# A two-layer encoder step: which engine begins the prompt attention's loads, and where one mixer keeps its cached values

## The chip, the core and the metric

The kernel runs on one core of a Trainium2 chip. The core has a matrix engine (PE), a vector engine (DVE), a scalar engine (ACT), a general engine (POOL) and a synchronising engine (SP) that here only begins transfers. Each works through its own list of instructions in order; a transfer between DRAM and on-chip memory (SBUF) is begun by an instruction in one of these lists and then carried out by the core's 16 DMA engines. The metric is the device time of one launch in microseconds, lower is better.

## The reference

Two request groups go through the same weights: one prompt of 512 frames and eight samples of 16 frames with 256 cached frames each. Layer 0 mixes by an RWKV recurrence beside forgetting attention (`fox`), layer 1 by chunk-band attention (`chunk`) beside an HGRN recurrence; a gated convolution network follows each. Cut to the attention:

```python
def fox_prompt(q, k, v, logf):                 # mixer 0, 8 heads of 64, 512 frames
    cum = jnp.cumsum(logf.astype(jnp.float32), axis=1)
    ...
        s = jnp.einsum('bqhd,bkhd->bhqk', qi, k) * ATTN_SCALE \
            + fi.transpose(0, 2, 1)[..., None] - f_keys      # f_keys: cum of the keys
        s = jnp.where(pi[:, None] >= pos[None, :], s, -jnp.inf)
        p = jax.nn.softmax(s, axis=-1)
        return jnp.einsum('bhqk,bkhd->bqhd', p, v)
def chunk_attn_prompt(q, k, v, rel_bias):      # mixer 1: the same with a bias by distance
    bias = rel_bias[:, jnp.clip(rel, -REL_CLIP, REL_CLIP) + REL_CLIP]
    s = jnp.einsum('bcqhd,bckhd->bchqk', qc, kb) * ATTN_SCALE + bias[None, None]
    ...
def chunk_attn_sample(q, k, v, ck, cv, rel_bias):   # 16 new frames over 256 cached ones
    keys = jnp.concatenate([ck, k], axis=1)
    vals = jnp.concatenate([cv, v], axis=1)
    ...
def trunk(x, c, P, cache):
    for layer in range(DEPTH):                 # DEPTH = 2
        h = rmsnorm(x) * (1.0 + scale) + shift
        y, st = ab_mixer(h, ...) if layer % 2 == 0 else cd_mixer(h, ...)
        x = x + gate * y
        h = rmsnorm(x) * (1.0 + scale) + shift
        y, buf_new = conv_ffn(h, ...)
        x = x + gate * y
```

All values are 32-bit floats.

## The kernel before

**Matrix products with weights.** `linear` (L334) takes the weights of a layer in steps of up to 512 KB. A step is loaded by SP into a ring of four tiles named `wraw` (L344, L345). ACT casts the tile to a rounded part `whi` (L348), DVE forms the remainder `wlo` (L349), and PE makes three products for each pair of weight block and half of the frames (L359, output `lin`). These are the bulk of the program.

**Prompt attention.** `attn_prompt` (L1027) goes through the eight heads in four pairs. Q, K and V of a mixer have been written to DRAM in parts. For each pair, twelve loads of 64 x 512 values (128 KB, L1072) bring Q and the two parts of K for both heads, one load (L1073) brings V, and `prep` brings one table per head: in mixer 0 the running sums of `logf`, spread over the partitions (L956, into `room`), in mixer 1 the distance bias `cbp` (L1406), which DVE then negates (L1407) and POOL masks in a corner (L1408). Before the change POOL begins the twelve and SP begins the V load and the tables. Every tile here exists once (`room`, L1012; the trace calls some of these tiles `ra`, the others `room`), so the next pair's loads wait until the last reader of the present pair is done. Within a pair, `front` makes the scores (PE, `qk`, L1044), adds the table and takes the extreme (DVE, L1045), the exponential (ACT, L1046) and the normalisation (DVE, L1047 and L1048); `turn` transposes the probabilities (PE, `ptr`, L1054) and copies them (ACT, L1055); `back` multiplies by V (PE, `av`, L1061), and DVE copies the result (L1063). The V of a pair is transposed once (PE, `vt`, L1084). `todo` lets `turn` and `back` run one block behind `front`, so that the last blocks of a pair are finished in the next pair.

**Sample attention.** `attn_sample` (L1093) takes the eight samples one after another. `front` loads a sample's cached keys `kc` and values `vc`, 512 KB each, from SP (L1121, L1122) into the same ring of four `wraw` tiles that the weights use, and makes the scores (`sqk`, L1129 and L1130). `back` runs one sample later and is the last to read `vc` (`sav`, L1152; its scaling on DVE is L1154, its transpose `syt` L1156).

**The recurrence of mixer 0.** For each stretch of frames it inverts a small triangular matrix by some 30 short POOL instructions that follow each other (L683 and L685, tiles `Tt` and `Ttmp`), with the operands going to DRAM and back before and after (tile `d`).

**What sets the order.** The program gives work in lanes with priorities, and a scheduler that simulates the engines' times sorts every engine's list (the class `Streams` holds the lanes). A change of who begins a transfer therefore moves other instructions too. In mixer 0 the prompt attention, the sample attention and the recurrence run beside the input product (`lin`), and beyond its end; in mixer 1 prompt attention, sample attention and HGRN run beside it.

**How a transfer is waited for.** Transfers begun by SP and ACT share a set of eight completion counters in this program (the ones begun by POOL have eight others); a transfer that reuses a counter is begun only when the one before it on that counter has landed. SP, ACT or POOL, whichever begins it, waits in its list, and what stands behind waits with it.

Of the kernel before, what the change touches and what calls it, by code (L numbers as in the profile page):

```python
# [9 lines left out]
F32 = mybir.dt.float32  # L10
# [9 lines left out]
NP = 512  # L20
# [119 lines left out]
H = (slice(0, 64), slice(64, 128))  # L140
# [374 lines left out]
def mixer0(tc, A, k):  # L515
    nc = tc.nc
    V, S, G, T, dma, mm, fm, P, C = k.V, k.S, k.G, k.T, k.dma, k.mm, k.fm, k.P, k.C
# [9 lines left out]
    with tc.tile_pool(name="mx", bufs=1) as mp:  # L527
# [419 lines left out]
        cumd = dr.tile([8, NP], F32, name="cumd")  # L947
# [5 lines left out]
        S.activation(ncq.rearrange("p a b -> p (a b)"), pst[:, 0:32], AF.Copy, scale=-1.0)  # L953

        def prep(head, t):
            dma(t, cumd[head].partition_broadcast(128))  # L956
            return t

        def addend(head, i, t, o):
# [67 lines left out]
def attn_prompt(A, k, mp, ydr, slot, dq, dk, dv, prep, addend, room):  # L1027
# [40 lines left out]
    for p in range(4):  # L1068
        for h in range(2):
            for (t, d) in ((qs[h], (dq[0], dq[1])), (kh[h], (dk[0], dk[0])), (kl[h], (dk[1], dk[1]))):  # L1070
                for g in range(2):
                    G.dma_start(t[H[g]], d[g][p][H[h], :NP])  # L1072
        dma(v, dv[p][:, :NP])  # L1073
        for h in range(2):
            prep(2 * p + h, cb[h])
        for i in range(4):
            front(p, i, 0)
            if todo is not None:
                turn(todo[1], 1)
                back(*todo)  # L1080
            if i == 0:
                ps = fm("vt", 1)
                for j in range(4):
                    T.transpose(ps[:, 128 * j:128 * j + 128], v[:, 128 * j:128 * j + 128], ident)  # L1084
                S.copy(vt.rearrange("p a b -> p (a b)"), ps)
            front(p, i, 1)
            turn(i, 0)
            todo = (p, i)
# [1 line left out]
    back(*todo)  # L1090


def attn_sample(A, k, mp, ydr, slot, dq, dk, dv, sprep, sbias, sadd, ck, cv, tags, bank):  # L1093

    V, S, G, T, dma, _, C, act = k.V, k.S, k.G, k.T, k.dma, k.lm, k.C, k.act
    ident = k.ident
# [19 lines left out]
    def front(b):  # L1116
        s_ = ss[b % 2]
        kc = k.wp.tile([128, 1024], F32, tag="wraw", name="kc", bufs=4)
        vc = k.wp.tile([128, 1024], F32, tag="wraw", name="vc", bufs=4)
        kc, vc = kc.rearrange("p (a t) -> p a t", a=4), vc.rearrange("p (a t) -> p a t", a=2)  # L1120
        dma(kc, A[ck][b])  # L1121
        dma(vc, A[cv][b])  # L1122
        ps = bank("sqk")
        if sbias is not None:
            sbias(b, ps)
        for p in range(4):
            lhs = qbd[:, p, b].rearrange("p h t -> p (h t)")
            o = ps[32 * p:32 * p + 32]
            T.matmul(o[:, 0:256], lhs, kc[:, p, :], start=sbias is None, stop=sbias is None, tile_position=(0, 32 * p))  # L1129
            T.matmul(o[:, 256:384], lhs, ks[:, p, :], start=sbias is None, stop=True, tile_position=(0, 32 * p))  # L1130
        st = mp.tile([128, 2], F32, tag="sst", name="sst", bufs=3)
        if sadd is not None:
            sadd(b, ps, s_, st)
            src = s_
        else:
            V.tensor_reduce(st[:, 0:1], ps[:, :384], axis=AX.X, op=ALU.min)
            src = ps[:, :384]
        S.activation(s_, src, AF.Exp, scale=-1.0, bias=st[:, 0:1], accum_out=st[:, 1:2])
        V.reciprocal(st[:, 1:2], st[:, 1:2])
        return b, s_, vc, st  # L1140
# [33 lines left out]
def mixer1(tc, A, k):  # L1174
# [13 lines left out]
    with tc.tile_pool(name="hx", bufs=1) as mp:  # L1188
# [214 lines left out]
        V.tensor_copy(C["win"][:, 112:128], sbt[:, 256:272])  # L1403

        def prep(head, t):
            dma(t, A["cbp"][head])  # L1406
            V.tensor_scalar(t, t, -1.0, None, op0=ALU.mult)  # L1407
            G.memset(t[0:64, 448:512], BIG)  # L1408
            return t
# [6 lines left out]
            V.tensor_tensor_reduce(s_[:, 256:384], ps[:, 256:384], C["win"][:, 112 - 16 * b:240 - 16 * b], 1.0, st[:, 1:2],  # L1416
                                   op0=ALU.add, op1=ALU.min, accum_out=st[:, 0:1])

        sample = k.stepper(1, attn_sample(A, k, mp, ydr, 0, cqs, cks, cv, lambda r: None, None, sadd, "c_ck", "c_cv", k.tags[0], mm), ln=1)
        lin([0, 1, 2, 3, 4, 5, 6, 7], (1,), sample)  # L1420
        sample.rest()
        with k.lane(1):
# [122 lines left out]
```

## Time and profile before

| | before |
|---|---|
| runs, us | 2049.37, 2043.58, 2048.91 (median 2048.91) |
| profiled execution, us | 2047.2 |
| its span, us | 2045.4 |
| granted TensorE clock, mean | 0.977 |
| PE / DVE / ACT / POOL busy | 94% / 59% / 46% / 26% |

The span runs from the first to the last record of the profiled execution; the other 1.8 us lie around it. The granted clock is a share of full speed (2.4 GHz); 0.977 is a mean over the span. A busy share is that of all instructions of an engine that have a duration; instructions that begin a transfer are not counted in it.

### The profile page before, as it was taken

The numbers are of one execution on the slowest core, as the hardware profiler recorded it, in microseconds if no ns is written. First come the engines' busy times: TensorE is split into PE (matmuls) and PEld (weight loads), VectorE is DVE, ScalarE is ACT, GpSimd is POOL, SyncE is SP. The second block draws the span as 40 slices with busy tenths as digits, with TensorE's granted clock in tenths as the row PEclk, the third lists the DMA queues.
The fourth block names the chain that finished last, engine by engine and source line by source line (L and its number), as shares of the span: only waits on it lengthen the run. The fifth ranks groups of instructions, "written<-read, shape, count | busy, mean of one in ns | idle before, by whom it ended". The sixth has DMA issues, their size and how long they took to land. (4 is left out here: it accounts for less than half of the span.)

```text
span 2045.4 us, 42529 instructions
## 1 busy us (share of the span) xinstructions
PE 1932.5 (94%) x16860; PEld 1746.0 (85%) x16860; DVE 1216.1 (59%) x2485; ACT 943.9 (46%) x1877; POOL 524.6 (26%) x1090
## 2 busy tenths in 40 slices
PE   5999998998999999999999999988999999999997
PEld 2877787765797899999999888877889999999997
DVE  3755665786686454454558515776678653454455
ACT  4634433454456451451446425565637642452454
POOL 1425453535021120121112201443222321121112
PEclk7999999998999999999999999999999999999998
DMA  8464436376535532222236775456634322222223
GB/s 314 146 224 122 158 116 188 92 180 167 160 121 184 198 112 78 78 66 79 79 102 214 242 247 175 124 141 185 218 95 152 108 75 81 73 67 78 83 80 124
DMA packets 144663, 282.52 MB, mean 138 GB/s; under 512 B 39769, under 2 KB 80065, under 8 KB 144465
## 3 DMA queue, kind: packets, MB, share of 16 engines
q1 hardware_dynamic: 136784, 267.22, 41.3%
q0 software_dynamic: 7680, 12.59, 2.9%
q8 instruction: 133, 2.18, 0.4%
q14 instruction: 66, 0.53, 0.1%
HBM read 247.69 MB, written 32.07 MB: 137 GB/s over the span
## 5 line engine op out<-in xcount | busy, mean ns | idle before, releaser
L359 PE MATMUL lin<-hi,whi 128*128 128x320 f32 x2272 | 716.1, 315 | 16.8 <-ACT whi L348 8.9
L359 PE MATMUL lin<-hi,wlo 128*128 128x320 f32 x2272 | 713.2, 314 | 5.8 <-DVE wlo L349 5.7
L359 PE MATMUL lin<-lo,whi 128*128 128x320 f32 x2272 | 711.7, 313 | 0.0
L349 DVE TENSOR_TENSOR wlo<-wraw,whi 128x1024 fp32r<-128x1024 f32 (+1 forms) x272 | 334.3, 1230 | 349.5 <-ACT whi L348 348.6
L348 ACT CAST whi<-wraw 128x1024 fp32r<-128x1024 f32 (+1 forms) x272 | 279.6, 1028 | 505.0 <-PE lin L359 373.4
L359 PEld LDWEIGHTS lin<-hi,whi 128*128 128x128 f32 x2272 | 431.0, 190 | 40.2 <-ACT whi L348 12.3
L359 PEld LDWEIGHTS lin<-hi,wlo 128*128 128x128 f32 x2272 | 430.8, 190 | 21.1 <-DVE wlo L349 9.0
L359 PEld LDWEIGHTS lin<-lo,whi 128*128 128x128 f32 x2272 | 430.9, 190 | 6.2 <-issue 2.7
L359 PE MATMUL lin<-gh,whi 128*128 128x320 f32 x704 | 218.1, 310 | 2.9 <-ACT whi L348 1.8
L359 PE MATMUL lin<-gl,whi 128*128 128x320 f32 x704 | 217.5, 309 | 0.6 <-DVE gl L451 0.6
L359 PE MATMUL lin<-gh,wlo 128*128 128x320 f32 x704 | 217.4, 309 | 0.6 <-DVE wlo L349 0.5
L433 POOL COPY cvo<-u 128x2 f32<-128x2 f32 x88 | 82.8, 941 | 383.4 <-ACT u L431 383.4
L394 DVE SCALAR_TENSOR_TENSOR x<-lin,ada_cm,x 128x192 f32<-128x192 f32 (+1 forms) x160 | 76.8, 482 | 143.5 <-PE lin L359 142.7
L359 PEld LDWEIGHTS lin<-gh,whi 128*128 128x128 f32 x704 | 132.0, 188 | 4.6 <-ACT whi L348 2.8
L359 PEld LDWEIGHTS lin<-gl,whi 128*128 128x128 f32 x704 | 132.1, 188 | 1.3 <-DVE gl L451 1.1
L359 PEld LDWEIGHTS lin<-gh,wlo 128*128 128x128 f32 x704 | 132.0, 188 | 1.4 <-DVE wlo L349 1.1
L399 POOL TENSOR_TENSOR x<-x,rs 128x128 f32<-128x128 f32 x80 | 49.7, 622 | 304.6 <-DVE rs L397 290.9
L437 DVE SCALAR_TENSOR_TENSOR t<-u,pp,t 128x656 f32<-128x656 f32 x88 | 79.3, 901 | 27.2 <-ACT t L436 26.6
L251 PE MATMUL ada<-wada,csT 128*32 128x256 f32 x768 | 70.2, 416 | 19.6 <-DMA wada<-in_ada_w_dram 19.3
L1294 POOL TENSOR_TENSOR d<-d,q 128x160 f32<-128x160 f32 (+1 forms) x48 | 41.7, 869 | 182.0 <-ACT d L1293 182.0
L359 PE MATMUL lin<-yh,whi 128*128 128x320 f32 x256 | 81.4, 321 | 5.5 <-DVE eL L1258 2.3
L436 ACT ACTIVATE t<-u,pp 128x656 f32<-128x656 f32 x88 | 82.6, 939 | 7.2 <-ACT u L432 0.4
(389 smaller groups left out, 3091.3 us busy)
## 6 DMA issues: line engine op xcount, KB each, us to landing
wraw<-in_w_up_dram SPq DMA_DIRECT2D x100, 512.0 KB
wada<-in_ada_w_dram SPq DMA_DIRECT2D x96, 512.0 KB
wraw<-in_w_cd_dram SPq DMA_DIRECT2D x44, 512.0 KB
wraw<-in_w_dn_dram SPq DMA_DIRECT2D x48, 448.0 KB
wraw<-in_w_ab_dram SPq DMA_DIRECT2D x40, 512.0 KB
wraw<-in_w_dn_dram SPq DMA_DIRECT2D x16, 512.0 KB
wraw<-in_w_abo_dram SPq DMA_DIRECT2D x12, 512.0 KB
wraw<-in_w_cdo_dram SPq DMA_DIRECT2D x12, 512.0 KB
```

What stands on the lines that cost most here:

```text
L251: T.matmul(ps[32 * j:32 * j + 32, 0:256], csT[:, kk, :], w[:, j * 256:(j + 1) * 256], start=kk == 0, stop=kk == KD - 1, tile_position=(0, ...
L348: S.copy(wh[:, :w], r[:, :w])
L349: V.tensor_tensor(wl[:, :w], r[:, :w], wh[:, :w].bitcast(F32), op=ALU.subtract)
L359: T.matmul(ps[:, 0:HF], w[:, (j * nk + kk) * 128:(j * nk + kk + 1) * 128], a(h, kk), start=c == 0, stop=c == 3 * nk - 1)
L394: V.scalar_tensor_tensor(xx[:, :npr], ps[:, :npr], m[:, 16 + o, 0:1], xx[:, :npr], op0=ALU.mult, op1=ALU.add)
L399: G.tensor_tensor(xx[:, npr:], xx[:, npr:], t.rearrange("p b t -> p (b t)"), op=ALU.add)
L433: G.tensor_copy(cvo[:, o, 0, :], u[:, NP:NP + 2])
L436: S.activation(t, u[:, 2:], AF.Identity, scale=pp[:, ow + 88 + o:ow + 89 + o], bias=pp[:, ob + o:ob + o + 1])
L437: V.scalar_tensor_tensor(t, u[:, 1:UW - 1], pp[:, ow + 44 + o:ow + 45 + o], t, op0=ALU.mult, op1=ALU.add)
L1294: G.tensor_tensor(dv[:, :, h2:], dv[:, :, h2:], xq[:, :, h2:], op=ALU.mult)
```

## The change

The twelve L1072 loads of each pair, its V load and its two tables are begun by ACT instead of POOL and SP, in both mixers: 96 loads leave POOL, 8 V loads and 16 tables leave SP, and ACT's list gets 120 instructions. The `bitcast` only matches the type of the destination. In mixer 1 the cached values `vc` of the samples get two tiles of their own (8 KB in each partition) and no longer pass through the `wraw` ring; the keys `kc` stay there. The amount of data is the same. From L1094 on the line numbers of the changed program are one higher.

```diff
--- before.py
+++ after.py
@@ -953,7 +953,7 @@
         S.activation(ncq.rearrange("p a b -> p (a b)"), pst[:, 0:32], AF.Copy, scale=-1.0)
 
         def prep(head, t):
-            dma(t, cumd[head].partition_broadcast(128))
+            S.dma_start(t, cumd[head].partition_broadcast(128))
             return t
 
         def addend(head, i, t, o):
@@ -1069,8 +1069,8 @@
         for h in range(2):
             for (t, d) in ((qs[h], (dq[0], dq[1])), (kh[h], (dk[0], dk[0])), (kl[h], (dk[1], dk[1]))):
                 for g in range(2):
-                    G.dma_start(t[H[g]], d[g][p][H[h], :NP])
-        dma(v, dv[p][:, :NP])
+                    S.dma_start(t[H[g]].bitcast(F32), d[g][p][H[h], :NP])
+        S.dma_start(v, dv[p][:, :NP])
         for h in range(2):
             prep(2 * p + h, cb[h])
         for i in range(4):
@@ -1090,7 +1090,7 @@
     back(*todo)
 
 
-def attn_sample(A, k, mp, ydr, slot, dq, dk, dv, sprep, sbias, sadd, ck, cv, tags, bank):
+def attn_sample(A, k, mp, ydr, slot, dq, dk, dv, sprep, sbias, sadd, ck, cv, tags, bank, own=False):
 
     V, S, G, T, dma, _, C, act = k.V, k.S, k.G, k.T, k.dma, k.lm, k.C, k.act
     ident = k.ident
@@ -1116,7 +1116,8 @@
     def front(b):
         s_ = ss[b % 2]
         kc = k.wp.tile([128, 1024], F32, tag="wraw", name="kc", bufs=4)
-        vc = k.wp.tile([128, 1024], F32, tag="wraw", name="vc", bufs=4)
+
+        vc = mp.tile([128, 1024], F32, tag="vc", name="vc", bufs=2) if own else k.wp.tile([128, 1024], F32, tag="wraw", name="vc", bufs=4)
         kc, vc = kc.rearrange("p (a t) -> p a t", a=4), vc.rearrange("p (a t) -> p a t", a=2)
         dma(kc, A[ck][b])
         dma(vc, A[cv][b])
@@ -1403,7 +1404,7 @@
         V.tensor_copy(C["win"][:, 112:128], sbt[:, 256:272])
 
         def prep(head, t):
-            dma(t, A["cbp"][head])
+            S.dma_start(t, A["cbp"][head])
             V.tensor_scalar(t, t, -1.0, None, op0=ALU.mult)
             G.memset(t[0:64, 448:512], BIG)
             return t
@@ -1416,7 +1417,7 @@
             V.tensor_tensor_reduce(s_[:, 256:384], ps[:, 256:384], C["win"][:, 112 - 16 * b:240 - 16 * b], 1.0, st[:, 1:2],
                                    op0=ALU.add, op1=ALU.min, accum_out=st[:, 0:1])
 
-        sample = k.stepper(1, attn_sample(A, k, mp, ydr, 0, cqs, cks, cv, lambda r: None, None, sadd, "c_ck", "c_cv", k.tags[0], mm), ln=1)
+        sample = k.stepper(1, attn_sample(A, k, mp, ydr, 0, cqs, cks, cv, lambda r: None, None, sadd, "c_ck", "c_cv", k.tags[0], mm, own=True), ln=1)
         lin([0, 1, 2, 3, 4, 5, 6, 7], (1,), sample)
         sample.rest()
         with k.lane(1):
```

Since the scheduler sorts the lists anew, three places show what else has moved. The first is DVE in mixer 1 at the change from the first pair of heads to the second; before, the negation of the second head's table (L1407) stands there ahead of the copy of the finished pair's result (L1063, `av`):

```order
L1047 RECIPROCAL st<-st 128x1
L1048 TENSOR_SCALAR ra<-ra,st 128x512
L1301 COPY_PREDICATED att<-hl,lev 128x320
L1407 TENSOR_SCALAR room<-room 128x512
L349 TENSOR_TENSOR wlo<-wraw,whi 128x1024
L1219 TENSOR_SCALAR sg<-z 128x320
L1063 COPY room<-av 128x128
```

Changed, the same stretch of DVE:

```order
L1047 RECIPROCAL st<-st 128x1
L1048 TENSOR_SCALAR ra<-ra,st 128x512
L1302 COPY_PREDICATED att<-hl,lev 128x320
L1063 COPY room<-av 128x128
L1220 TENSOR_SCALAR sg<-z 128x320
L349 TENSOR_TENSOR wlo<-wraw,whi 128x1024
L1408 TENSOR_SCALAR room<-room 128x512
```

The copy of `av` now stands ahead of the remainder `wlo`, of the sigmoid step (`sg`) and of the negation, which is L1408 here.

The second is POOL in mixer 0, in the next to last of its eight chains of `Tt`, where the loads of the third pair (DRAM sides `fk`, `fq`) fall into the chain:

```order
L683 TENSOR_TENSOR Ttmp<-Tt,At 40x48
L1072 DMA ra<-fk_226 64x512 x2
L685 TENSOR_TENSOR Tt<-Tt,Ttmp 40x4x12
L1072 DMA ra<-fq_218 64x512
L1072 DMA ra<-fq_222 64x512
L1072 DMA ra<-fk_230 64x512 x2
L683 TENSOR_TENSOR Ttmp<-Tt,At 40x55
L1072 DMA ra<-fk_226 64x512 x2
L1072 DMA ra<-fq_218 64x512
L1072 DMA ra<-fq_222 64x512
L1072 DMA room<-fk_230 64x512 x2
L685 TENSOR_TENSOR Tt<-Tt,Ttmp 40x5x11
```

Changed, POOL in the same chain:

```order
L683 TENSOR_TENSOR Ttmp<-Tt,At 40x48
L685 TENSOR_TENSOR Tt<-Tt,Ttmp 40x4x12
L683 TENSOR_TENSOR Ttmp<-Tt,At 40x55
L685 TENSOR_TENSOR Tt<-Tt,Ttmp 40x5x11
L683 TENSOR_TENSOR Ttmp<-Tt,At 40x60
```

The loads are gone from POOL, and the chain stands without a break.

The third is ACT in mixer 0, from the last blocks of the second pair on; before there is no transfer:

```order
L1055 COPY ra<-ptr 128x512
L1138 ACTIVATE r_6621,sst<-sqk,sst 128x384
L1147 COPY r_6621<-sptr 128x384
L1055 COPY room<-ptr 128x512
L635 ACTIVATE e_5553<-cum 128x320
L1046 ACTIVATE ra,st<-ra,st 128x128
L636 ACTIVATE s<-s 128x320
L637 ACTIVATE cum<-cum 128x320
```

Changed, ACT over the same last blocks:

```order
L845 COPY y<-Ys 128x128
L1072 DMA ra<-fk_226 64x512
L1055 COPY ra<-ptr 128x512
L1072 DMA ra<-fq_218 64x512
L1046 ACTIVATE ra,st<-ra,st 128x512
L1072 DMA ra<-fq_222 64x512
L1072 DMA ra<-fk_226 64x512
L1072 DMA room<-fk_230 64x512
L850 ACTIVATE sq_4506<-y 128x320
L1072 DMA room<-fk_230 64x512
L1148 COPY r_6621<-sptr 128x384
```

The loads of the third pair now stand between the copies of the transposed probabilities (L1055), the exponentials (L1046) and the sample's copy (`sptr`, L1148 here, L1147 before). What waits behind a load on ACT is now one of these.

## Rows read from the trace of the kernel before

**Rows 1.** The page: busy time by engine, and the chain that ended last.
```profile
PE 1932.5 (94%) x16860; PEld 1746.0 (85%) x16860; DVE 1216.1 (59%) x2485; ACT 943.9 (46%) x1877; POOL 524.6 (26%) x1090
...
PE lin L359 24%; DVE nt L317 0%; DMA yb<-zdr 0%; PE lev L1271 0%; ACT whi L348 0%; DVE wlo L349 0%; DVE lo L324 0%; PE st L303 0%; ACT yh L509 0%; DVE nt L496 0%; PE KVs L1336 0%; DMA out_dram<-nt 0%; PE Os L1346 0%; ACT rstd L306 0%; ACT rstd L307 0%
```
**Rows 2.** Busy by stretch: start:end, length, PE, PEld, DVE, ACT, POOL, PE clock, DMA, GB/s.
```profile
330.00:560.00 230.00, 203.43 (x2384) 154.13 (x2383) 159.46 (x470) 107.75 (x280) 90.81 (x214) 0.94 0.58 156
1240.00:1460.00 220.00, 198.09 (x2468) 173.00 (x2469) 158.89 (x465) 132.04 (x315) 66.57 (x108) 0.95 0.57 169
340.00:350.00 10.00, 4.81 (x31) 4.29 (x32) 7.69 (x24) 2.77 (x5) 5.64 (x12) 0.90 1.13 244
350.00:360.00 10.00, 10.00 (x79) 9.37 (x79) 2.26 (x6) 3.07 (x8) 2.54 (x5) 0.76 0.55 162
1290.00:1300.00 10.00, 5.99 (x102) 5.42 (x100) 3.67 (x10) 4.18 (x9) 2.47 (x6) 0.85 0.68 146
1300.00:1310.00 10.00, 10.00 (x103) 9.52 (x102) 8.61 (x27) 8.91 (x23) 7.85 (x11) 0.81 0.23 80
1390.00:1400.00 10.00, 5.55 (x45) 4.24 (x38) 5.04 (x16) 3.35 (x7) 0.81 (x4) 0.66 1.11 296
1440.00:1450.00 10.00, 7.15 (x65) 5.91 (x66) 5.94 (x15) 5.90 (x12) 0.00 (x0) 0.86 0.96 325
```
**Rows 3.** The same of L359 alone: PE, PEld, clock, DMA, GB/s.
```profile
400.00:530.00 130.00, 0.00 (x0) 0.00 (x0) 0.92 0.71 187
1240.00:1460.00 220.00, 99.67 (x576) 90.87 (x577) 0.95 0.57 169
```
**Rows 4.** Timeline, first change of pairs in mixer 1: start, duration, [idle before, releaser].
```profile
1290.42 0.33 SPq L1406 DMA_DIRECT2D room<-in_cbp_dram  x1
...
1296.33 0.43 DVE L1407 TENSOR_SCALAR room<-room 128x512 f32<-128x512 f32 x1 [3.98 <-DMA room<-in_cbp_dram]
...
1298.04 0.28 DVE L1063 COPY room<-av 128x128 f32<-128x128 f32 x1
...
1298.38 1.12 PE L1054 MATMUL ptr<-c_ident,ra 128*128 128x128 f32 x4 [4.01 <-DVE room L1063]
```
**Rows 5.** Timeline, the third pair of mixer 1: DVE, then PE.
```profile
1392.83 0.43 DVE L1407 TENSOR_SCALAR room<-room 128x512 f32<-128x512 f32 x1 [3.52 <-DMA room<-in_cbp_dram]
...
1394.17 0.48 PE L1156 MATMUL syt<-c_ident,r 128*128 128x128 f32 x1 [3.85 <-DVE r L1154]
```
**Rows 6.** Waits over the whole span: who, for whom, us in all, times, longest.
```profile
POOL ra L1072 <- PE qk L1044: 26.5, 6, 12.4
...
DVE room L1407 <- DMA room<-in_cbp_dram: 12.8, 6, 4.0
...
PE lin L359 <- ACT whi L348: 10.6, 11, 2.6
```
**Rows 7.** Waits of SP's own list.
```profile
SPq L1406 <- DVE st L1045: 24.0, 6, 7.7
SPq L1122 <- PE sqk L1130: 23.4, 4, 11.8
```
**Rows 8.** Instructions of L1072 and L1073: count, duration ns min/median/max, first and last start.
```profile
L1072 POOL DMA_DIRECT2D ra<-ck x24: 517/557/737, 1156.4 to 1387.8; - x24
...
DMA to landing us min/median/max: 2.4/4.3/9.8
...
L1073 SPq DMA_DIRECT2D ra<-fv x4: 319/372/469, 341.1 to 460.9; - x4
```
**Rows 9.** Timeline of PE, first pair of mixer 0, and fourth.
```profile
341.98 0.41 PE L359 MATMUL lin<-hi,whi 128*128 128x320 f32 x1 [2.03 <-DVE f L1023]
...
496.01 0.36 PE L1044 MATMUL qk<-ra 128*128 128x256 f32 x1 [1.35 <-DMA ra<-fq]
```
**Rows 10.** Waits of PE for V's transfer.
```profile
PE vt L1084 <- DMA ra<-fv: 3.2, 1, 3.2
```
**Rows 11.** Timeline of POOL around a chain of `Tt`.
```profile
442.47 1.10 POOL L1072 DMA_DIRECT2D ra<-fk  x2 [0.19 <-PE trB L733]
...
448.88 1.07 POOL L1072 DMA_DIRECT2D room<-fk  x2
...
487.65 1.10 POOL L1072 DMA_DIRECT2D ra<-fk  x2 [12.38 <-PE qk L1044]
```

## The prediction

> **What bounds the kernel now.** I read the page's busy shares and its chain first. PE is busy for 94% of the span, and the chain that ended last is made of `lin`, the weight products [rows 1]. So a gain can only come from stretches in which PE stands still or runs at a low clock, and a loss from anything that keeps PE from its next product. Next I read the busy time by stretch at the two places where prompt attention runs [rows 2]. In mixer 0, 330 to 560 us, PE is busy 203.4 of 230 us: 26.6 us idle. In mixer 1, 1240 to 1460 us, it is busy 198.1 of 220: 21.9 us idle. The mean granted clock there is 0.94 and 0.95 against 0.977 for the whole span. The ceiling of what a change of these loads can give is therefore about 48 us of idle time and 0.06 × 230 + 0.05 × 220 = 25 us of clock, 74 us in all. The clock falls after PE's standstills: in 1290 to 1300 PE is busy 6.0 us and the clock is 0.85, and in the next 10 us, when PE is full again, it is 0.81; the same at 340 to 360 with 0.90 and then 0.76. A stop of PE costs itself and about as much again in slow products.
>
> What is there to fill PE differs between the mixers. In mixer 0 no `lin` product is left between 400 and 530 us, in mixer 1 it makes 99.7 us of the stretch [rows 3]. So in mixer 1 a late table can be covered by weight products if the order of the lists allows it, in mixer 0 only by the recurrence and the samples.
>
> Then I looked at which wait ends last at PE's stops. In mixer 1 at the first change of pairs the second table is begun at 1290.42, and DVE waits 3.98 us for it at L1407 until 1296.33. The remainder `wlo` and the sigmoid step come next, then the copy of `av` at 1298.04, for which PE had been waiting 4.01 us, although that copy needs nothing of the table [rows 4]. At 1392.8 the same: DVE waits 3.52 us at L1407, and PE 3.85 us for a DVE instruction (L1154) queued behind it [rows 5]. Over the span DVE waits 12.8 us at L1407 [rows 6]. So these stops are a matter of DVE's order and of when the table is begun, not of the twelve loads.
>
> **The change part by part**, against the profiled execution's own 2047.2 us, which is 1.7 us under the median of the runs, 2048.9.
>
> *First change of pairs, mixer 1.* In the changed order of DVE the copy of `av` stands ahead of `wlo`, the sigmoid step and the negation. PE then gets its `av` bank back before DVE waits for the table. That takes away the 4.0 us stop and the clock lost with it, (0.15 + 0.19) × 10 = 3.4 us [rows 2, 4]. Bounds: 0 (another wait takes its place) to −7.4. The scheduler's order is known here and the releaser is named, so I take −7.4. What is late next: the second head's scores, whose table is first read at the next block's L1045, when weight products stand on PE.
>
> *Later changes of pairs, mixer 1.* Around 1390 and 1440 PE is idle 4.45 + 2.85 us and loses (0.34 + 0.14) × 10 = 4.8 us of clock, 12.1 together [rows 2]. Two things act there. Counted in PE's list, 134 weight products stand between the V transpose of the last pair and its last scores in the changed program, and 59 before, so PE has more to put into the gaps. And `vc` leaves the ring: SP waited 23.4 us for `sqk` before it could begin L1122 [rows 7], with the next weight steps behind it. That ring's lateness reaches PE only as L348's waits, 10.6 us in the whole program [rows 6]. Bounds 0 to −12.1; I take a third, −4.0, as the reads of the samples still come in bursts (DMA share 1.11 at 1390 [rows 2]).
>
> *First pair of mixer 0.* V's transfer was late by 3.2 us [rows 10], in the stretch that ends in the slow clock of 340 to 360, (0.10 + 0.24) × 10 = 3.4 us [rows 2]. On ACT it now stands first, ahead of the twelve loads. The data are written to DRAM only just before (PE's other wait there, 2.03 us, is for DVE's part of the same products [rows 9]), and 13 transfers then want the DMA engines at once (share 1.13). Between 0 and −6.6 I take half, −3.3.
>
> *POOL rid of its loads.* 96 × 0.55 = 53 us of POOL go [rows 8]. POOL is 26% busy, so only chains matter in which loads cut the `Tt` steps. From 442.47 to 449.95 twelve loads stand in one such chain, 12 × 0.55 = 6.6 of these 7.5 us [rows 8, 11]; in the changed order none do. PE has no `lin` then and is 88% busy, so a part of the chain's lead reaches it. Bounds 0 to −7.5; a quarter, −1.9.
>
> *ACT's new load.* The trace has no transfer begun by ACT. Nearest rows: SP begins one in 0.33 to 0.37 us [rows 4, 8], POOL in 0.55 [rows 8]. I take SP's 0.33, as its kind of transfer is the one that ACT begins: 120 × 0.33 = 40 us of ACT, at the upper end 66 us. ACT is busy 108 of 230 and 132 of 220 us there [rows 2], so with about half of it nothing stands behind that is urgent; of the other 20 us I let a quarter reach PE through late exponentials, copies of `ptr` and casts `whi`: +5. Bounds: 0 (all in ACT's gaps) and +33 (half of 66, all on the path).
>
> *Waits in front of the loads.* Counted in the changed program, of ACT's 120 transfers 48 wait for a transfer begun by SP and 34 for an earlier one of ACT on the same completion counter. A load lands in 4.3 us at the median and 9.8 at the most [rows 8], so a counter that was used longer ago than that is free when ACT comes to it; where one is not, the exponential or the copy behind the load on ACT waits, and `ptr` and `av` on PE wait for that. From the other side, POOL stood 26.5 us in six waits for the last reader `qk`, the longest 12.4 [rows 6, 11], at little cost, since only `Tt` steps and other loads stood behind it. On ACT the scheduler has put the loads between exponentials that depend on nearly the same products, so the wait for `qk` should be mostly over when ACT gets there. Bounds 0 and +20 (three quarters of 26.5); I take +3.
>
> The trace shows what a list that waits costs: SP stood 24.0 us in front of L1406 for DVE's last read of the old table, up to 7.7 us at a time, and the next weight step behind it waited too [rows 7]. The Trainium skill ("Perfetto Trace Analysis", sections "DMA Instruction — HWDGE (DVE, Sync)" and "DMA Instruction — SWDGE (GPSIMD)") says the same of SP's kind of transfer: the semaphore wait sits in the sequencer of the engine, while on GpSimd the instruction is pushed into a wait queue. By that rule, taken alone, the loads would hold ACT for as long as their buffers are busy, which is the slower rival below; the 26.5 us of POOL in this trace show that here POOL's list was held as well, so the rule's second half finds no support in it.
>
> *Sum:* −7.4 − 4.0 − 3.3 − 1.9 + 5 + 3 = −8.6. 2047.2 − 8.6 = 2038.6, and beside the median of before, 1.7 higher, 2040.3; I say 2040.
>
> **The rivals.**
>
> *ACT is held as POOL was (slower).* The loads of a pair wait on ACT for the last `qk` of the pair before, as on POOL: 26.5 us [rows 6], plus some 4 us of counters; behind them stand `whi` casts, for which PE waited 10.6 us already, and the copies of `ptr`. In mixer 0 there is no weight product to cover it. If two thirds reach PE, +20, with +5 for the beginnings and half of the gains above, −8: +17, 2064 beside the median. It decides from the point where the wait for the reader's end is longer than 3 us in more than four of the eight pairs. For it: 82 of 120 loads wait for a counter, and ACT has work that PE needs, POOL had not. Against it: exponentials that stand before these loads need the same `qk`.
>
> *Nothing changes.* The loads land no sooner, since the same bytes go over the same 16 DMA engines right after the same readers; the gaps stay with another name, and the gains in DVE's order (−7.4, −4.0) meet the cost of ACT (+8). That gives −3 or so at most, 2046 to 2049. The Trainium skill ("DMA: Bandwidth & Descriptors", section "Issuing engines are not separate DMA queues") supports this: transfers of all issuing engines run on the same 16 DMA engines, so a change of issuer saves only the time that it takes to begin them. The DMA share of 1.11 and 1.13 where pairs start [rows 2] agrees with it.
>
> *Much more.* With the tables, V and the loads begun early and out of the way of SP's weight steps, half of the idle time and of the lost clock in mixer 1 goes (17 us) and a third of mixer 0's 40: −17 − 13 + 5 = −25, 2024 beside the median. For it: the clock comes back with each closed gap. Against it: PE's remaining idle is spread over dozens of short waits.
>
> **How the numbers follow.** Small gain 0.42, much more 0.12, nothing 0.20, slower 0.26. A measurement of this kernel can tell about 0.3%, 6.1 us, from no change. The small gain's own range is 2032 to 2045, of which four fifths lie under 2042.8. Faster: 0.12 + 0.34 = 0.46; within 0.3%: 0.08 + 0.20 = 0.28; slower 0.26. The range reaches down to the much larger gain's 2024 and up to 2062, just under the held ACT's 2064.
>
> **What would show it.** Right: no idle DVE at the negation in front of the copy of `av`; PE's stop near 1294 gone and the clock around it at 1.0; PE's wait for V's transfer gone; ACT's busy time unchanged while its own idle time before L1072 stays under 10 us in all; POOL's `Tt` chains without breaks. Wrong: PE waiting for ACT's `ptr` copies, exponentials or `whi` for more than 10 us longer than now, or ACT standing for `qk` in front of L1072 for more than 15 us; then it is slower. If PE's stops at the pairs are as long as before with a transfer as releaser, it is no change.

## The result, and the profile after

| | before | changed |
|---|---|---|
| median of 6 runs each, us | 2044.9 (2034.3 to 2049.4) | 2061.7 (2059.1 to 2063.9) |
| ratio to before | 1 | 1.0073, 95% interval 1.0046 to 1.0100 |
| the same in two later sessions | 1 | 1.0064 (1.0040 to 1.0089) and 1.0060 (1.0040 to 1.0079) |
| span of the profiled execution, us | 2045.4 | 2058.2 |
| granted clock in it | 0.977 | 0.971 |

By the ratio the change makes the kernel 12 to 15 us slower; the forecast was 8.6 us less. Measured times below are ratios to runs of the kernel before on the same chip, turned into microseconds with 2045 us, with a 95% interval in brackets.

The page of the changed kernel, busy time by engine, and the lines of two queues of transfers (packets, MB, share of the DMA engines):

```profile
PE 1948.9 (95%) x16860; PEld 1756.2 (85%) x16860; DVE 1213.4 (59%) x2485; ACT 943.9 (46%) x1877; POOL 465.1 (23%) x994
...
q1 hardware_dynamic: 133328, 260.93, 39.7%
q10 hardware_dynamic: 11136, 18.88, 3.4%
```

Before there is no q10; SP's queue and POOL's then:

```profile
q1 hardware_dynamic: 136784, 267.22, 41.3%
q0 software_dynamic: 7680, 12.59, 2.9%
```

By its bytes q10 is ACT's: it has the 12.59 MB of POOL's q0 and the 6.29 MB of V and the tables that left SP's q1. POOL has lost its 96 instructions and 59 us [rows 1]; DVE's and ACT's busy time is as before. PE has the same 16,860 products and is busy for 16 us more: the products take longer. Most of that is the clock. One minus the granted clock, times the span, is what an execution loses to half clock; in these two profiled executions it is 13.7 us more. Over all timed runs the changed kernel lost 59, 57 and 56 us on the mean of its three sessions, the kernel before 48 to 50. In the two later sessions that is 8 us of the 13.1 and of the 12.3.

**Where it lies.** A single profiled execution differs from the next by several microseconds in its clock alone, so I cut all executions at the same products of `lin` (the start of the 500th, 1000th, ... L359 product) and took means over those whose PE list is the same in a mixer, but for a handful of rows. Each entry is length / idle time of PE / time lost to half clock, in us:

```
stretch of lin       lists of before      lists of the change   mixer 0 on SP
0 to 500             173.6 / 28.9 / 14.3   171.3 / 26.8 / 14.0   174.1 / 28.7 / 15.4
500 to 1000          137.5 /  0.4 /  0.0   151.7 /  4.9 /  3.8   137.1 /  0.0 /  0.0
1000 to 1250         228.7 / 25.4 / 13.0   230.2 / 19.3 / 17.1   222.8 / 18.2 /  7.4
1250 to 1750          93.0 /  4.8 /  0.7    88.1 /  7.5 /  3.1    87.1 /  6.0 /  0.6
mixer 0, sum         632.8 / 59.5 / 28.0   641.3 / 58.5 / 38.0   621.1 / 52.9 / 23.4
4500 to 6500 (mixer 1) 492.9 / 31.1 / 11.1   501.4 / 34.6 / 14.2
```

(Mixer 0: five executions each for before and the change, three for SP, from the experiments below; mixer 1: four and three.) In mixer 0 PE stands still no longer than before, 58.5 against 59.5 us, but loses 10 us more to the clock; in mixer 1 both rise by 3 us. The two mixers give +8.5 us each, 17 in all: the result, within what a few executions can say. In mixer 0 the executions overlap, 625 to 640 us before and 634 to 652 changed; in mixer 1 they do not, 489 to 496 and 498 to 504.

The surprising row is the second. The loads of Q, K and V begin behind it (the first at 353 us), and yet PE, which had next to no idle time there, now has 5 us. Not all of the row's 14 us is loss: between the 500th and the 1000th `lin` product the changed list has 104 more products of PE than the list before (1574 against 1470), and the last row has 152 fewer. Busy time by stretch (columns as in [rows 2]) of the changed kernel, inside it and at the end of the mixer:

```profile
270.00:280.00 10.00, 8.19 (x116) 6.27 (x114) 3.44 (x10) 3.45 (x8) 8.28 (x29) 0.94 0.36 106
280.00:290.00 10.00, 10.00 (x38) 7.89 (x37) 3.39 (x7) 4.79 (x10) 4.93 (x13) 0.55 0.18 27
...
550.00:560.00 10.00, 5.55 (x23) 4.72 (x23) 5.01 (x12) 2.98 (x7) 0.32 (x8) 0.76 0.77 235
```

and of the kernel before:

```profile
270.00:280.00 10.00, 10.00 (x124) 7.67 (x122) 3.41 (x9) 5.00 (x12) 8.59 (x30) 1.00 0.28 90
280.00:290.00 10.00, 10.00 (x79) 7.80 (x80) 6.98 (x14) 5.87 (x13) 6.52 (x17) 1.00 0.44 126
```

After a standstill of 1.8 us the clock is at 0.55 of full speed in the next 10 us, nearly all of it at the lower of the two levels, and 38 products (in part other ones) get done where 79 did. That is one execution of many: eight of the profiled ones have this stop, of 1.5 to 2.2 us, and behind it the lower clock lasted between 0 and 10 us. The timeline of the changed kernel, DVE and then PE, shows the stop:

```profile
277.56 0.46 DVE L884 SCALAR_TENSOR_TENSOR zs<-d,pp,z 128x192 f32<-128x192 f32 x1 [3.25 <-POOL d L883]
277.94 0.39 DVE L885 SCALAR_TENSOR_TENSOR zs<-d,pp,z 128x128 f32<-128x128 f32 x1
278.36 0.28 DVE L795 SCALAR_TENSOR_TENSOR St<-St,eL,Sn 128x64 f32<-128x64 f32 x1
...
276.20 0.68 PE L750 MATMUL U<-SAV,ABM 64*64 64x64 f32 x16
278.70 0.37 PE L741 MATMUL SA<-St,W 64*64 64x64 f32 x2 [1.81 <-DVE St L795]
...
555.80 0.90 PE L359 MATMUL lin<-yh,whi 128*128 128x320 f32 x2 [4.11 <-ACT yh L509]
```

The same place before:

```profile
276.66 0.46 DVE L884 SCALAR_TENSOR_TENSOR zs<-d,pp,z 128x192 f32<-128x192 f32 x1 [2.54 <-POOL d L883]
277.04 0.39 DVE L885 SCALAR_TENSOR_TENSOR zs<-d,pp,z 128x128 f32<-128x128 f32 x1
277.46 0.28 DVE L795 SCALAR_TENSOR_TENSOR St<-St,eL,Sn 128x64 f32<-128x64 f32 x1
...
276.45 0.68 PE L750 MATMUL U<-SAV,ABM 64*64 64x64 f32 x16
277.06 0.80 PE L606 MATMUL w<-zlr,w2a 64*128 64x320 f32 x2
...
280.53 0.33 PE L741 MATMUL SA<-St,W 64*64 64x64 f32 x4
```

DVE waits for POOL and then makes `St` within 0.9 us of the same time in both. Before, PE's list has `w`, `a` and eleven products of `lin` between `U` and `SA`, which needs `St`; in the changed list `SA` stands right behind `U`. No transfer that the change moved is near. The list is another one, from the 312th product of `lin` on, and the first row of ACT's list that differs is the first pair of table loads (L956) at 101 us.

At the places that the prediction spoke of, the waits did go. DVE and PE of the changed kernel, first change of pairs in mixer 1:

```profile
1300.63 0.29 DVE L1063 COPY room<-av 128x128 f32<-128x128 f32 x1
1305.38 0.42 DVE L1408 TENSOR_SCALAR room<-room 128x512 f32<-128x512 f32 x1
...
1303.47 0.66 PE L1054 MATMUL ptr<-c_ident,ra 128*128 128x128 f32 x4
```

Neither waits, where both stood for 4 us [rows 4]. But other waits of PE came; the changed kernel over its whole span:

```profile
PE lin L359 <- ACT yh L509: 7.0, 3, 4.1
PE lin L359 <- ACT whi L348: 6.5, 7, 2.6
...
PE qk L1044 <- DMA ra<-ck: 2.7, 1, 2.7
```

`yh` is the input of the mixers' output product, 0.5 us before. On means over the executions of the table, in us: PE's waits in mixer 1 for `room` (3.7) and before `syt` (3.8) went, and most of that for `whi` (6.2 to 2.4); new or longer are those for `yh` (3.5), for a key load before `qk` (3.7), for POOL's `d` (3.7 to 6.6), before `sav` (0.2 to 2.4) and for `x` (0.1 to 2.8). In mixer 0 the waits for V's transfer (3.3), for Q before `qk` (2.0) and before `W` (3.1) went, and most of that for `f` (5.3 to 0.7); new or longer are those before `Ss` (3.4), for K before `qk` (3.4), for `yh` (0.7 to 2.8) and before `Sn` (1.7).

ACT's own list, the first pair of mixer 0 in the changed kernel (ACTq: its sequencer beginning transfers), and the row of PE that needs the copy behind the loads:

```profile
354.69 3.11 ACTq L1072 DMA_DIRECT2D ra<-fk  x4
357.84 2.25 ACTq L1072 DMA_DIRECT2D ra<-fq  x2
360.14 1.25 ACTq L1072 DMA_DIRECT2D ra<-fk  x2
361.43 0.43 ACT L807 COPY y<-Y 128x320 f32<-128x320 f32 x1 [6.92 <-DMA ra<-fq]
...
361.91 0.81 PE L606 MATMUL mean<-y,blkr 128*128 128x320 f32 x2 [0.18 <-ACT y L807]
```

ACT's engine did nothing for 6.9 us in front of the copy, most of it while loads were being begun. But the product `Y` that it copies ended only at 360.80, so the copy came 0.6 us late, and PE waited 0.18 us for it. In all, the 120 beginnings took 66 us of ACT, not 40. In front of them ACT's list waited 21 us more (24 and 17 in two other executions), 17 of them for landings and under 2 for `qk`. PE's waits for ACT, added up over the span, were 21.6 us before and are 30.1 to 31.8 in three executions of the change; its waits for DVE fell from 53.5 us to 34 to 39. Whether ACT is the loss is what the experiments had to tell.

### The profile page after: what moved, and what is told of

The parts are those of the page before. It is cut to its first block, busy times and chain, and to the rows that moved or that the text cites. A ratio compares the mean times of both kernels' runs of the same rounds, so it can differ in the third digit from the quotient of the medians.

```text
span 2058.2 us, 42410 instructions
## 1 busy us (share of the span) xinstructions
PE 1948.9 (95%) x16860; PEld 1756.2 (85%) x16860; DVE 1213.4 (59%) x2485; ACT 943.9 (46%) x1877; POOL 465.1 (23%) x994
## 4 chain that ended last, share of the span: by engine, by line
PE 65%; issue 10%; DMA 9%; DVE 9%; POOL 3%; ACT 3%; SPq 1%; ACTq 0%; POOLq 0%; DVEq 0%
PE lin L359 54%; DMA wada<-in_ada_w_dram 2%; DVE wlo L349 1%; PE ada L251 1%; POOL Ttmp L683 1%; POOL Tt L685 1%; PE lev L1272 1%; DVE nt L317 1%; ACT whi L348 1%; DMA TB<-d 1%; PE qk L1044 1%; PE av L1061 1%; DMA room<-cumd 1%; DMA wraw<-in_w_ab_dram 1%; PE ptr L1054 1%
## 5 line engine op out<-in xcount | busy, mean ns | idle before, releaser
L359 PE MATMUL lin<-hi,whi 128*128 128x320 f32 x2272 | 717.4, 316 | 5.8 <-ACT whi L348 4.7
L359 PE MATMUL lin<-hi,wlo 128*128 128x320 f32 x2272 | 713.1, 314 | 4.3 <-DVE wlo L349 4.2
L359 PE MATMUL lin<-lo,whi 128*128 128x320 f32 x2272 | 710.4, 313 | 0.0
L359 PEld LDWEIGHTS lin<-hi,whi 128*128 128x128 f32 x2272 | 430.8, 190 | 31.3 <-issue 9.2
L359 PEld LDWEIGHTS lin<-hi,wlo 128*128 128x128 f32 x2272 | 430.8, 190 | 18.1 <-issue 6.8
L359 PEld LDWEIGHTS lin<-lo,whi 128*128 128x128 f32 x2272 | 431.1, 190 | 6.7 <-issue 4.0
L359 PE MATMUL lin<-gh,whi 128*128 128x320 f32 x704 | 219.6, 312 | 2.9 <-ACT whi L348 1.8
L359 PE MATMUL lin<-gh,wlo 128*128 128x320 f32 x704 | 218.7, 311 | 1.0 <-DVE wlo L349 0.9
L359 PE MATMUL lin<-gl,whi 128*128 128x320 f32 x704 | 218.9, 311 | 0.6 <-DVE gl L451 0.6
L359 PEld LDWEIGHTS lin<-gh,whi 128*128 128x128 f32 x704 | 133.2, 189 | 4.8 <-ACT whi L348 2.8
L359 PEld LDWEIGHTS lin<-gh,wlo 128*128 128x128 f32 x704 | 133.3, 190 | 1.9 <-DVE wlo L349 1.8
L359 PEld LDWEIGHTS lin<-gl,whi 128*128 128x128 f32 x704 | 133.3, 189 | 1.3 <-DVE gl L451 1.1
L359 PE MATMUL lin<-yh,whi 128*128 128x320 f32 x256 | 81.7, 323 | 10.8 <-ACT yh L509 7.0
L427 ACT COPY u<-lin 128x320 f32<-128x320 f32 x88 | 37.5, 427 | 98.2 <-PE lin L359 98.2
```

Source lines behind the costliest of these rows:

```text
L359: T.matmul(ps[:, 0:HF], w[:, (j * nk + kk) * 128:(j * nk + kk + 1) * 128], a(h, kk), start=c == 0, stop=c == 3 * nk - 1)
L427: S.copy(u[:, 2:2 + HF], ps)
```

## The experiments

Theory A: ACT is held at its transfers and what is queued behind comes late. Its first rival, B with D: the scheduler sorts all lists anew, and the new order and the clock decide, whoever begins the loads.

**Parts of the change.** Mixer 0 alone (`slot` is 4 in mixer 0 and 0 in mixer 1; V and the tables are chosen alike), the loads of mixer 1 alone, and the own tiles alone. One line of the first:

```diff
-                    G.dma_start(t[H[g]], d[g][p][H[h], :NP])
+                    (S if slot == 4 else G).dma_start(t[H[g]].bitcast(F32) if slot == 4 else t[H[g]], d[g][p][H[h], :NP])
```

> The change in mixer 0 alone (its 60 transfers on ACT, mixer 1 and the cached values as before). Theory A, that ACT is held at its loads and what stands behind them comes late: the input product and mixer of layer 0 end 8 us later, as in the profile of the whole change (its 1750th weight product 8.0 us later than before), so about +8 to +12 us in all. Rival B, that the loss is the clock's and the start's, not of the loads (13.8 us more were lost to half clock in the whole change, 5.2 of them in the first 50 us): within 4 us of before. Rival C, that the cached values' own tiles cost it: 0 here.

> The change of the loads in mixer 1 alone (60 transfers on ACT), the cached values still in the weights' ring, mixer 0 as before. Theory A: mixer 1 loses less than mixer 0, as weight products cover part of it; +2 to +6 us. Rival B: within 4 us of before. Rival C, that the cached values' own tiles are what costs: 0 or a gain of some 5 us here, since the order on DVE alone is mended.

> Only the two own tiles for the cached values of mixer 1; all loads begun as before. Theory A: a gain of 0 to 4 us, as the ring is freed. Rival B: 0. Rival C: slower by 5 us or more, since SP then begins weight and cached-value loads earlier and they take the DMA engines from the pair's loads.

Measured: +2.7 us (−0.8 to 6.1), +6.3 (2.9 to 9.8), +3.7 (−0.6 to 8.2). Each part is a small loss or none; none carries the 12 to 15 us. Theory A's +8 for mixer 0 was missed here. Own tiles alone bring nothing, against what the prediction hoped of the ring.

**SP in place of ACT**, the whole change with `dma(...)`, which is SP, for `S.dma_start(...)`:

> The whole change, but all 120 transfers begun by SP instead of ACT. Theory A: ACT is free again, so most of the 16 us go; what SP's waits cost instead falls on the weights' loads, which are four steps ahead: between -3 and +6 us against before. Rival B, that the loss comes with any new order of the lists and the clock: as slow as the whole change, +12 to +18.

Measured −1.4 us (−5.5 to 2.7), as theory A has it. Beginning the 96 loads took SP as long as it took ACT (56.5 us against 56.3), so the cost would lie in whose list is held, not in the beginnings. The next runs did not bear A out.

**How many on ACT.** Half of the loads on SP (72 transfers on ACT); V and the tables on SP (96); only V and the tables on ACT (24); all of mixer 1's part with own tiles (60). One line of the first of the four:

```diff
-                    S.dma_start(t[H[g]].bitcast(F32), d[g][p][H[h], :NP])
+                    (S.dma_start if h == 0 else dma)(t[H[g]].bitcast(F32), d[g][p][H[h], :NP])
```

> The whole change, but of the twelve loads of a pair six (the first head's) are begun by ACT and six (the second head's) by SP; V and the tables stay on ACT: 72 transfers on ACT instead of 120. Theory A, that ACT's list is what is paid for (66 us of beginning transfers and some 27 us of standing at landings in the whole change, against 0 with all on SP, which came out at -1.5 us): the loss goes with the number on ACT, about half of the 16 us, +5 to +10. Rival D, that the order into which the scheduler sorts everything decides and ACT only happened to get a bad one: anything between -8 and +16, without relation to the share on ACT.

> The whole change without V and the tables: the 96 loads on ACT, the 8 of V and the 16 tables on SP as before, the cached values in their own tiles. Theory A: nearly all of the loss, +10 to +16, as 96 of 120 are still on ACT. Rival E, that the tables and V are what holds ACT, since they wait for DVE's and PE's last reads: most of the loss gone, 0 to +5.

> The counterpart: only V and the tables on ACT (24 transfers), the 96 loads on POOL as before, the cached values in their own tiles. Theory A: the effect of the own tiles alone (+4) and a fifth of the rest, +4 to +7. Rival E: +10 or more.

> All that the change does in mixer 1 (60 transfers on ACT and the own tiles), mixer 0 as before. If the parts add up: +6 (loads of mixer 1 alone) and +4 (own tiles alone), together +10, and with +3 of mixer 0 alone nearly the whole 16. If the own tiles pay only together with the loads, as the prediction had it: under +6.

Measured: +0.4 us (−4.1 to 4.9), +13.1 (6.7 to 19.6), +5.7 (0.8 to 10.6), +1.6 (−3.1 to 6.3). 96 transfers cost as much as 120, 72 cost nothing, 24 cost 6 us: the time does not go with the number on ACT.

**The whole again, and ACT's beginnings alone**, with twelve small transfers for each pair that nothing reads (`c` counts the three tiles of a head):

```diff
                     G.dma_start(t[H[g]], d[g][p][H[h], :NP])
+                    S.dma_start(small[H[g], 8 * (6 * h + 2 * c + g):8 * (6 * h + 2 * c + g) + 8], d[g][p][H[h], :8])
```

> The whole change once more, unaltered. Its lists in mixer 0 are those of the run with mixer 0 alone (+3 us), its lists in mixer 1 those of the run with all of mixer 1's part (-1 us), so the two parts should make about +2 us together; six runs of the whole gave +16. If the parts add up (theory F: the first six runs and their three of before overstate it): +1 to +8 us. If the mixers work on each other, for instance through the transfers' counters and the clock (theory G): +12 to +18 again.

> The kernel before, with twelve more, very small transfers for each pair (64 x 8 values, into a tile that nothing reads) begun by ACT beside POOL's twelve loads: ACT's beginnings and their counters alone, 96 of them, without moving a load. Theory A: ACT's time for beginning (about 0.55 us each, 53 us) and its standing at counters are what costs: +5 to +12. Theory D (only the order of the lists): within 4 us of before, of either sign.

Measured +13.1 us (8.2 to 18.2) and +8.0 (3.5 to 12.7). The second falls into A's range and outside D's. By its place it does not bear A out: in its one profile mixer 0, with 48 more transfers on ACT, took 622 us, 11 less than before, and mixer 1, with 48 more, 513 us, 20 more. It settles nothing between A and D.

**All of mixer 0 on SP**, mixer 1 as before:

```diff
-                    G.dma_start(t[H[g]], d[g][p][H[h], :NP])
+                    (dma(t[H[g]].bitcast(F32), d[g][p][H[h], :NP]) if slot == 4 else G.dma_start(t[H[g]], d[g][p][H[h], :NP]))
```

> All 60 transfers of mixer 0 begun by SP, mixer 1 as before. In the profile of the kernel with everything on SP mixer 0 took 9 us less than before once the slow clock is taken off, and mixer 1 nothing: if that holds, -5 to -9 us, a version faster than both. If it was one lucky execution: within 3 us of before.

Measured 0.9925 (0.9902 to 0.9949), −15.3 us (−20.0 to −10.4): faster than both kernels, and by more than expected. Its stretches, in an execution of 2024.4 us, one of the fastest of its twelve (median 2031.6):

```profile
270.00:280.00 10.00, 10.00 (x133) 8.19 (x129) 4.45 (x11) 4.53 (x11) 8.27 (x29) 1.00 0.36 107
...
310.00:530.00 220.00, 201.67 (x2602) 147.49 (x2601) 157.64 (x486) 108.05 (x284) 69.45 (x174) 0.98 0.57 168
530.00:620.00 90.00, 83.22 (x579) 78.18 (x578) 67.08 (x140) 47.34 (x90) 19.59 (x38) 1.00 0.41 131
```

The longest of them in the kernel before:

```profile
310.00:530.00 220.00, 195.40 (x2394) 145.04 (x2391) 153.16 (x455) 102.92 (x271) 91.13 (x221) 0.94 0.62 166
```

The early part is as before, without a stop. Behind it PE stands for 18 us instead of 25, and the clock is 0.98 instead of 0.94.

**The eight tables of mixer 0**, found as the first difference of the lists: they alone on ACT, and the whole change without them:

```diff
-            S.dma_start(t, cumd[head].partition_broadcast(128))
+            dma(t, cumd[head].partition_broadcast(128))
```

(this is the second; the first is the kernel before with the line reversed)

> The kernel before with one edit: the eight tables of mixer 0 (L956) begun by ACT, 8 transfers of 120. The first two of them stand on ACT about 100 us into the program, and PE's list differs from there on. Theory H, that this new order of mixer 0's recurrence is where the loss starts: the stretch between the 500th and the 1000th weight product, which took 149.9 to 153.3 us in the five executions profiled with these tables on ACT and 137.0 to 137.9 us in the seven with them on SP and no further transfer added to ACT, takes 149 to 153 here, PE stands there for 5 us instead of 0.3, and the whole is +4 to +10. Theory A (ACT's time at its loads): 8 of 120 transfers, within 2 us of before, and the stretch as before.

> The whole change, but the eight tables of mixer 0 stay on SP; 112 transfers on ACT. Theory H: the stretch between the 500th and the 1000th weight product is 137 us again and some 8 us of the 13 to 16 go: +3 to +8. Theory A: nearly nothing goes, +11 to +16, as 112 of 120 transfers are still on ACT.

Measured +2.0 us (−1.4 to 5.5) and +0.2 (−4.1 to 4.3). Without the eight tables 112 of 120 transfers are on ACT and the loss is gone, all of it: theory A falls. It falls by its own measures too. In this run ACT's list waited 23 us in front of its loads and PE 30.4 us for ACT, as in the whole change, at no loss; with the 96 loads alone on ACT it was 12.5 and 24.6 us, at a loss of 13.1. The stretch has no stop any more:

```profile
270.00:280.00 10.00, 10.00 (x140) 7.80 (x139) 4.69 (x14) 4.18 (x10) 7.57 (x27) 1.00 0.37 111
280.00:290.00 10.00, 10.00 (x69) 7.40 (x69) 5.59 (x13) 6.22 (x14) 7.01 (x21) 1.00 0.30 77
```

Theory H is right about the place: with the tables alone on ACT the stretch took 148.6 us with 5.1 us idle. It is not right about the price: that run gets the time back in later stretches (223.6 and 87.0 us, 5 and 6 less than before), and behind the same stop its clock did not fall:

```profile
270.00:280.00 10.00, 8.47 (x115) 6.29 (x112) 3.99 (x10) 4.82 (x12) 8.51 (x31) 1.00 0.17 55
280.00:290.00 10.00, 10.00 (x76) 7.79 (x76) 8.06 (x17) 6.07 (x15) 5.82 (x11) 1.00 0.45 124
```

So taking the tables off ACT takes the loss off this change, and the tables alone do not make it. Nor does a loss need them: the run with the 96 loads alone on ACT had these tables on SP and no stop here (137.2 us), and lost 13.1 us all the same, with 242.6 us from the 1000th to the 1250th product in its one profile, 14 more than before.

**A combination:** mixer 0 on SP, mixer 1 with its loads on ACT, V and tables on SP, own tiles:

> A version that might beat all: mixer 0 with all 60 transfers on SP (-13 us with mixer 1 as before), mixer 1 with its 48 loads on ACT, V and tables on SP and the cached values in their own tiles, whose mixer 1 took 488.9 us in its one profile against 495.6 on the mean of the executions with mixer 1 of before. If both add: -16 to -20. If the one profile was luck: -10 to -14.

Measured 0.9966 (0.9948 to 0.9984), −7.0 us (−10.6 to −3.3). Faster than before, but less than either expectation, and half of what mixer 0 on SP brought alone. In its profile mixer 1 was short again (485.9 us), so that the gain of the one profile was luck is not shown; nor is that mixer 0 on SP is worth 15 us each time.

**A control and the sum of the halves.** K's loads ahead of Q's in the kernel before, on the same engines, and the two halves again with the whole on one chip. The control's edit:

```diff
-            for (t, d) in ((qs[h], (dq[0], dq[1])), (kh[h], (dk[0], dk[0])), (kl[h], (dk[1], dk[1]))):
+            for (t, d) in ((kh[h], (dk[0], dk[0])), (kl[h], (dk[1], dk[1])), (qs[h], (dq[0], dq[1]))):
```

> A control: the kernel before, with K's eight loads of a pair ahead of Q's four; the same transfers by the same engines. The scheduler sorts the lists anew from the 1122nd weight product on (1173 of some 11,000 rows of PE's list differ). Theory D, that new orders by themselves move the time: anything up to 8 us of either sign, and different stretches from before. Theory A: within 2 us.

> The change in mixer 0 alone once more (first time +2.7 us). If the parts add up to the whole: +5 to +8, since its profile had mixer 0 8 us longer than the mean of before. If the whole is more than its parts: 0 to +4.

> All of the change in mixer 1 once more (first time +1.6 us by the ratio). If the parts add up to the whole: +4 to +8. If the whole is more than its parts: -2 to +3.

> The whole change on the same chip as its two halves: +13 to +16 as in both runs before. The sum of the two halves of this call against it tells whether they add up.

Measured: the control +6.7 us (3.1 to 10.4); mixer 0 +7.4 (3.7 to 11.0), mixer 1 +5.7 (1.6 to 9.8), the whole +12.3 (8.2 to 16.2). Here the halves add up, 13.1 against 12.3, though the half with mixer 1 has a few of its PE rows in another order than the whole. In the earlier sessions they made 4.3 against 13 to 15, and each half is known to some 4 us, so this stays open. The control shows that a new order, with no transfer on another engine, can move the time by half of what the change does. It is not an order of the lists alone, since the loads themselves come in another order: in its one profile PE's waits for Q and K before `qk` changed from 2.0 to 3.7 us, those before `Sn` and `SA` from 4.7 to 7.8.

## Why the prediction was wrong

- *What bounds the kernel* held: PE is the bound, and time is lost to its stops and to slow products. That a stop costs about as much again in slow products did not hold: the clock took 0.47 of PE's idle time in mixer 0 before and 0.65 in the change, 0.36 and 0.41 in mixer 1, and behind one and the same stop between nothing and 5 us. In mixer 0 10 us of clock came with no new idle time at all.
- *First change of pairs in mixer 1*, −7.4 us: the wait went exactly as the order showed it. *Later changes*, −4.0: `syt`'s wait went and `whi`'s fell by 3.8 us. *V in mixer 0*, −3.3: gone. *POOL's chains*, −1.9: whole again. But as terms of the sum, −16.6 together, they failed: each took a removed wait as time gained, and PE's idle time is not shorter afterwards (59.5 and 58.5 us in mixer 0, 31.1 and 34.6 in mixer 1). The bound at 0 was written down for each, for the first as "another wait takes its place", and then not chosen.
- *ACT's new load*, +5, was priced from SP's 0.33 us; the 64 x 512 loads took ACT 0.59 us (56.3 us for 96), and all beginnings 66 us, the upper end. *Waits in front of the loads*, +3: ACT's list waited 21 us, 17 of them for landings, and the wait for `qk` was indeed mostly over (under 2 us). Both terms had too little time on ACT. For what reached PE their +8 was about right, as PE's waits for ACT grew by 8.5 to 10 us. It is not what decides: the run without the eight tables has the same waits and no loss. The Trainium skill ("Perfetto Trace Analysis", "DMA Instruction — HWDGE (DVE, Sync)") has the wait in the sequencer, and the trace agrees for ACT: its list waited up to 2.8 us for a landing in front of one of these loads.
- The step that failed is the *sum* itself: it was made over the places where the loads of a pair stand, with the rest of the program taken as unchanged, so that each removed wait counted in full. The order shown ahead of the prediction covered three such places. The comparison of the lists from the start would have shown PE's list leave that of before at the 312th product, behind the first two tables and 250 us ahead of the first load of Q, K or V, over all of the recurrence. A term for that was missing. The runs with new lists in one mixer, and the control, give its size: +2 to +7 us, and −15 with SP in mixer 0. The prediction's signs looked at the same places: DVE's order, V's wait, ACT's busy time and POOL's chains came out as it wrote, neither sign of being slower did, and the kernel was slower. What the runs showed in place of the gain is other waits of PE of about the same length in all, and some 8 us more lost to half clock.
- The *slower rival*, ACT held, gave 2064 (its +17 makes that beside the profiled 2047.2, and 2066 beside the median that it names). The time of 2061.7 came near it by luck: ACT did not stand for `qk`, and PE's waits for `whi` and the copies of `ptr`, its price, became shorter (12.4 us before, 8.7 changed, over the span). *Nothing changes* was right in one thing: the Trainium skill's rule ("DMA: Bandwidth & Descriptors", "Issuing engines are not separate DMA queues") that another issuer saves only the time to begin. The trace agrees as far as that goes: 54 us of beginnings left POOL and 56 came to ACT. But here the issuer also changes the order of everything else: the 60 transfers of mixer 0 gave −15 us on SP and +3 to +7 on ACT.

What stays open is the cause in the strict sense. That the time goes with the number of transfers on ACT, or with ACT's waits, is refuted. That the new order of the lists decides is argued from this and from the first row that differs; no run had one order with two engines beginning the loads. Open too is why this order loses more to the clock, and whether SP's gain in mixer 0 is more than a lucky order. Three executions with SP there, in programs that differ in mixer 1, agree to 6 us (618.0 to 623.6 up to the 1750th product), but they share one order, and the three programs measured −15.3, −7.0 and −1.4 us.

## What to carry to other kernels

Where a scheduler sorts the lists, a change of who begins a transfer can change the order of everything behind it, here from the first two tables on: compare the lists from the first differing row on, and put a term of either sign for all that stands between there and the edit. Price a removed stop as a gain only if the engine's list has nothing else that waits soon after. And when a change moves the time by less than a percent, run a control that only reorders before believing any mechanism.

## What the runs showed of the hardware that was not expected

- Beginning a 64 x 512 transfer costs SP as much as ACT and a little more than POOL (means of 0.59, 0.59 and 0.56 us for the 96), and up to 1.73 us on ACT; a 128 x 512 one cost SP 0.36 on the mean of eight (L956).
- A standstill of 1.8 us was followed by 10 us at the lower clock, and the same stop in other executions by none or by 3 to 10 us. PE's idle time did not tell the loss: with 1 us less of it in mixer 0, 10 us more went to the clock.
- Executions of the kernel before spread by 17 to 30 us in a session (2038.5 to 2055.6 in 35 runs, 2030.3 to 2060.3 in 28), mostly by the clock: in the second of these 41 to 68 us were lost to half clock. With a dozen runs against some 30 of before the interval is 7 to 10 us wide.
